# Three more groups of the modulation products on TensorE, in a two-block kernel on one core

## The chip, the cores and the metric

The kernel runs on one core of a Trainium2 chip. The metric is the device time of one execution in microseconds; smaller is better. A core has five engines with an instruction queue each: TensorE (PE; its weight loads are shown as PEld), VectorE (DVE), ScalarE (ACT), GpSimd (POOL) and SyncE (SP), which here only issues the large loads. All run their own queue in order and wait for each other on semaphores.

## The reference

A token stream x (256 tokens, width 1024) goes through two layers of a first block and one layer of a second; a context stream of 256 tokens goes beside it. Each layer begins with modulation vectors that depend on a conditioning vector alone:

```python
mod = (jax.nn.silu(c) @ ada_w[i] + ada_b[i])[:, None, :]
sh1, sc1, g1, sh2, sc2, g2 = jnp.split(mod, N_MOD, axis=-1)
hx = modulate(rms_norm(x, norm_mix[i]), sh1, sc1)      # h * (1 + scale) + shift
...                                                    # the same with c_ctx for the context
m_lat, m_ctx = hybrid_mixer(hx, hc, ...)               # layer 0: attention heads beside a state-space scan
x = x + g1 * m_lat
x = x + g2 * swiglu(modulate(rms_norm(x, norm_ffn[i]), sh2, sc2), ...)
```

Layer 1 has a short convolution in place of the hybrid mixer. The second block does the same with its own weights (w_mod_2), a mixer of two linear recurrences and a mixture of experts. Each modulation product is a vector of 1024 against a matrix of 1024 × 6144 in fp32, 24 MB; there are three matrices. Only the shift and scale ahead of the first mixer of each block are wanted for c and for c_ctx; all others for c alone.

## The kernel before

**The modulation products.** A matrix is taken in three groups of 2048 columns, so there are nine groups (m, s): m is the matrix (0 and 1 for the two layers of the first block, 2 for the second block) and s the third of its columns. A group is eight tiles of 128 rows by 2048 columns, 1 MB each, one for each eighth (kt) of the contraction. `gemv(m, s)` loads a tile into the buffer `raw` and multiplies it in one of two ways. With `both` true, TensorE multiplies it by `csil`, 128 × 32 with silu(c) and silu(c_ctx) in its first two columns, and adds up over the eight tiles in a bank `gv`; the four slices of 512 columns go to four groups of 32 output partitions (four matmuls in the program, eight records in the trace). With `both` false, VectorE multiplies the tile by a column of `csil` and adds it to an accumulator `gva` of 128 × 2048, in two halves (L331 for the first tile, L333 for the others), and four matmuls against ones at the end of the group sum over the partitions, into the same kind of bank. In both cases L341 adds the bias on VectorE and gives `gvr`. `gv_cols` transposes `gvr` to columns, `gv_row` writes a gate to memory, from where `bc_row` reads it back.

**Who asks for them.** `gemv` is a generator: it yields after each tile. The first group (0,0) runs at the start. The others come in the order (0,1), (0,2), (2,0), (1,0), (1,1), (1,2), (2,1), (2,2), a tile at a time, where `pump` is called: some calls between the input projections of the first mixer (`hybrid`), three for each of its sixteen attention heads until the scan `ssd` is done, and after that together with the context side of the second block, beside the output projection, the first feed-forward part and so on. A scheduler then puts the instructions of each engine in an order of its own; loads on SP stay in the order in which the program asks for them.

**The buffers.** `raw` has three buffers, shared by the tiles of the modulation products and all slices of weights of the first block and the context side. A slice of weights is split into two halves of higher and lower bits (`split_to`: L243 on ScalarE and VectorE, into `whl`, three buffers), and three products (`mm3`) take the place of one. A load waits until the buffer's last reader is done.

**The mixer around it.** The slices of hy_w_in come in the order of the convolution part (bands of `xbc`), k and v, q, and z. For each head TensorE makes the scores `sc`, VectorE the maximum `nb`, ScalarE the exponential `e` with its sum `l`, VectorE the scaling (L714), TensorE four transposes of `e` (L731); four heads share a product `pv`. Beside them the scan has products `st`, `rb` and `yo`, and elementwise work on `g`, `mf`, `mb`, `xw` on VectorE. After the heads the norm of the context stream (`dg`, `hf`), its first projections (`c_hi`, `c_lo`) and the output projection (`mt_hi`, `mt_lo`) follow on TensorE.

Of the kernel before, what the change touches and what calls it, by code (L numbers as in the profile page):

```python
# [141 lines left out]
def tile_model(ctx: ExitStack, tc: tile.TileContext, aps: dict, out: bass.AP, dbg=None):  # L142
# [46 lines left out]
    def bank(name="b", tag=None):  # L189
        t = tag or tagsel[0]  # L190
        return psum["pool"].tile([P, 512], F32, tag=t, name=name, bufs=psum["tags"][t])
# [30 lines left out]
    def mm(o, l, r, start=True, stop=True):  # L222
        return nc.tensor.matmul(o, l, r, start=start, stop=stop)  # L223
# [86 lines left out]
    def gemv(m, s):  # L310

        w, cn = MATS[m]
        both = s == 0 and m != 1
        for i in range(1 + both):
            nc.gpsimd.dma_start(gvb[i:i + 97:32, :], aps["bias"][m, s])
        o = bank("gv", "G") if both else None
        acc = None if both else gvp.tile([P, 2048], F32, tag="gva", name="gva", bufs=1)
        for kt in range(KT):  # L320
            raw = ring.tile([P, 2048], F32, tag="raw", name="raw", bufs=NRAW)
            dmas.append(nc.sync.dma_start(raw, w[kt * P:(kt + 1) * P, s * 2048:(s + 1) * 2048]))
            if both:
                for g in range(4):
                    mm(o[32 * g:32 * g + 32, :], csil[cn][:, kt, :], raw[:, g * 512:(g + 1) * 512], kt == 0,
                       kt == KT - 1)
            else:
                for h in range(2):
                    c = slice(h * 1024, (h + 1) * 1024)
                    if kt == 0:  # L330
                        nc.vector.tensor_scalar(acc[:, c], raw[:, c], csil[cn][:, kt, 0:1], None, op0=ALU.mult)  # L331
                    else:
                        nc.vector.scalar_tensor_tensor(acc[:, c], raw[:, c], csil[cn][:, kt, 0:1], acc[:, c],  # L333
                                                       op0=ALU.mult, op1=ALU.add)
            yield
        if not both:
            o = bank("gv", "G")
            for g in range(4):
                mm(o[32 * g:32 * g + 32, :], ones[:, :32], acc[:, g * 512:(g + 1) * 512])
        r = gvp.tile([P, 512], F32, tag="gvr", name="gvr", bufs=1)  # L340
        nc.vector.tensor_add(r, o, gvb)  # L341
        return r
# [30 lines left out]
    def mods(m, parts):  # L373

        for i in parts:
            r = yield from gemv(m, i)
            if i == 0:
                MOD[f"c1_{m}"] = gv_cols(r, 1 if m == 1 else 2, f"ma{m}")
            elif i == 1:
                MOD[f"g1_{m}"] = gv_row(r, 0, f"g1_{m}")  # L380
                MOD[f"sh2_{m}"] = gv_cols(r, 1, f"mb{m}")[0][:, 8:16]
            else:
                MOD[f"sc2_{m}"] = gv_cols(r, 1, f"mc{m}")[0][:, 0:8]
                MOD[f"g2_{m}"] = gv_row(r, 1, f"g2_{m}")
# [1719 lines left out]
```

## Time and profile before

| | |
|---|---|
| time, median of 3 runs | 1550.29 us (1550.26 to 1551.28) |
| the profiled execution | 1556.02 us, of it the span from first to last instruction 1554.2 |
| TensorE busy | 1407.8 us (91%), 8039 matmul records |
| VectorE busy | 955.1 us (61%) |
| ScalarE busy | 634.8 us (41%) |
| GpSimd busy | 157.3 us (10%) |
| granted TensorE clock, mean | 0.943 of full speed |
| read from HBM | 317.37 MB |

The profile comes from one execution; its engines' busy times say nothing yet of who waits for whom. The granted clock has two levels, 1.00 (2.4 GHz) and 0.50 (1.2 GHz); a value between them is a mean over a stretch. A busy time at the lower level holds half the work. Times in the rows below are microseconds from the start of the span, unless marked ns.

### The profile page before, as it was taken

How to read it: one execution, taken by the hardware profiler on the slowest of the kernel's cores; microseconds unless marked ns; L12 is line 12 of the kernel's file. 1: busy time of each engine (PE TensorE's matmuls, PEld its weight loads, DVE VectorE, ACT ScalarE, POOL GpSimd, SP SyncE). 2: the span in 40 equal slices, each digit the busy share in tenths (PEclk: the TensorE clock that was granted, in tenths of full speed). 3: DMA queues.
4: the chain of work that ended last, by engine and by line, in shares of the span. 5: the costliest groups of instructions: out<-in, count | busy, mean ns of one | idle time of the engine just before them, and what ended most of it. 6: DMA issues, size and time to landing. Idle time of an engine off the chain costs nothing. (4 is left out here: it accounts for less than half of the span.)

```text
span 1554.2 us, 20809 instructions
## 1 busy us (share of the span) xinstructions
PE 1407.8 (91%) x8039; PEld 1061.2 (68%) x8039; DVE 955.1 (61%) x1526; ACT 634.8 (41%) x1020; POOL 157.3 (10%) x213
## 2 busy tenths in 40 slices
PE   4988698999999999999999997988899897989996
PEld 2666445677787798997788886888797753444442
DVE  1577869786888977755455566799944532223232
ACT  2643234554555435344444444864641411111211
POOL 2013220000001000001000000134402100000000
PEclk9997798999999999999999997999897978999998
DMA  9444558787789842443355552323210696999990
GB/s 353 161 152 139 200 209 307 245 293 260 268 279 328 299 154 96 136 136 130 128 189 189 180 182 94 128 83 108 82 55 1 229 340 227 362 358 388 393 355 29
DMA packets 133471, 320.35 MB, mean 206 GB/s; under 512 B 6632, under 2 KB 25064, under 8 KB 124112
## 3 DMA queue, kind: packets, MB, share of 16 engines
q1 hardware_dynamic: 130848, 311.31, 56.8%
q0 software_dynamic: 2480, 7.16, 1.3%
q8 instruction: 86, 1.41, 0.4%
q14 instruction: 57, 0.47, 0.1%
HBM read 317.37 MB, written 1.07 MB: 205 GB/s over the span
## 5 line engine op out<-in xcount | busy, mean ns | idle before, releaser
L243 DVE TENSOR_TENSOR whl<-raw,whl 128x1024 fp32r<-128x1024 f32 x252 | 311.1, 1242 | 179.2 <-ACT whl L243 178.7
L243 ACT CAST whl<-raw 128x1024 fp32r<-128x1024 f32 x252 | 261.8, 1047 | 320.2 <-PE b L223 115.3
L223 PE MATMUL gu<-whl,f_hi 128*128 128x512 f32 (+1 forms) x768 | 230.4, 383 | 1.8 <-DVE whl L243 1.8
L223 PEld LDWEIGHTS gu<-whl,f_hi 128*128 128x128 f32 x768 | 139.6, 189 | 34.7 <-DVE whl L243 3.4
L223 PE MATMUL gu<-whl,f_lo 128*128 128x512 f32 (+1 forms) x384 | 144.3, 377 | 0.0
L333 DVE SCALAR_TENSOR_TENSOR gva<-raw,csil,gva 128x1024 f32<-128x1024 f32 x98 | 123.4, 1291 | 16.9 <-DMA raw<-in_ada_w_dram 16.7
L223 PE MATMUL do<-whl,th 128*128 128x512 f32 x352 | 114.0, 400 | 0.3 <-DVE whl L243 0.2
L223 PE MATMUL gu<-mw,xg 128*64 128x512 f32 x384 | 91.7, 629 | 13.4 <-PEq L1964 11.2
L223 PEld LDWEIGHTS gu<-whl,f_lo 128*128 128x128 f32 x384 | 72.6, 189 | 14.2 <-issue 0.5
L223 PE MATMUL b<-l_hi,whl 128*128 128x256 f32 x384 | 75.4, 296 | 5.5 <-DVE whl L243 5.5
L223 PEld LDWEIGHTS gu<-mw,xg 128*64 128x64 f32 x384 | 32.7, 144 | 69.7 <-issue 65.7
L223 PEld LDWEIGHTS do<-whl,th 128*128 128x128 f32 x352 | 65.8, 188 | 17.0 <-DVE whl L243 1.8
L223 PE MATMUL b<-s_hi,whl 128*128 128x256 f32 x384 | 73.3, 287 | 0.0
L223 PE MATMUL do<-whl,tl 128*128 128x512 f32 x176 | 69.1, 396 | 0.0
L223 PEld LDWEIGHTS b<-l_hi,whl 128*128 128x128 f32 x384 | 61.9, 196 | 8.4 <-DVE whl L243 5.9
L223 PEld LDWEIGHTS b<-s_hi,whl 128*128 128x128 f32 x384 | 60.4, 189 | 0.7 <-issue 0.7
L223 PE MATMUL b<-whl,l_hi 128*128 128x512 f32 x160 | 52.8, 409 | 5.5 <-DVE whl L243 4.1
L1930 DVE SCALAR_TENSOR_TENSOR yf<-dn,gs,gbc 64x512 f32<-64x512 f32 (+1 forms) x36 | 25.9, 720 | 51.8 <-PEq L1964 47.7
L1282 DVE SCALAR_TENSOR_TENSOR qkv<-raw,cols_sb,qkv 128x189 f32<-128x189 f32 (+3 forms) x112 | 56.6, 551 | 0.0
L1891 DVE TENSOR_TENSOR sl<-sl,gu 128x256 f32<-128x256 f32 (+1 forms) x17 | 7.0, 413 | 79.4 <-ACT sl L1890 79.4
L223 PE MATMUL b<-l_lo,whl 128*128 128x256 f32 x192 | 55.6, 290 | 0.0
L223 PE MATMUL b<-s_lo,whl 128*128 128x256 f32 x192 | 54.9, 286 | 0.0
(549 smaller groups left out, 2723.6 us busy)
## 6 DMA issues: line engine op xcount, KB each, us to landing
raw<-in_ada_w_dram SPq DMA_DIRECT2D x48, 1024.0 KB, 5.1
raw<-in_w_in_dram SPq DMA_DIRECT2D x28, 1024.0 KB, 4.9
raw<-in_w_mod_dram SPq DMA_DIRECT2D x24, 1024.0 KB, 5.0
mw<-in_w_gate_dram SPq DMA_DIRECT2D x48, 512.0 KB, 12.2
mw<-in_w_up_dram SPq DMA_DIRECT2D x48, 512.0 KB, 11.5
raw<-in_ffn_w_gate_dram SPq DMA_DIRECT2D x22, 1024.0 KB, 5.1
raw<-in_ffn_w_up_dram SPq DMA_DIRECT2D x22, 1024.0 KB, 5.0
mw<-in_w_down_dram SPq DMA_DIRECT2D x22, 1024.0 KB, 11.9
```

The lines of the kernel that those rows point to most:

```text
L223: return nc.tensor.matmul(o, l, r, start=start, stop=stop)
L243: return nc.scalar.copy(hi, src), nc.vector.tensor_sub(lo, src, f32(hi))
L333: nc.vector.scalar_tensor_tensor(acc[:, c], raw[:, c], csil[cn][:, kt, 0:1], acc[:, c], op0=ALU.mult, op1=ALU.add)
L1282: nc.vector.scalar_tensor_tensor(yy, ov[:, r0 + dr:r1 + dr, c0 + dc:c1 + dc], c[:, 3 * a + b:3 * a + b + 1], yy, op0=ALU.mult, op1=ALU.add)
L1891: s2 = nc.vector.tensor_mul(sl[:, :c], sl[:, :c], o[:, c:2 * c])
L1930: nc.vector.scalar_tensor_tensor(yv, o[v, :c], gs[v, :], g2[v, n * c:(n + 1) * c], op0=ALU.mult, op1=ALU.mult)
```

## The change

Whether a group goes to TensorE is decided by the flag `both`. It was true for (0,0) and (2,0), the two groups that are wanted for both vectors. It is now true for (0,1), (0,2) and (1,0) too. The number of bias loads, which hung on `both`, now has the old condition written out, so it stays as it was.

```diff
         w, cn = MATS[m]
-        both = s == 0 and m != 1
-        for i in range(1 + both):
+        both = (m, s) in ((0, 0), (0, 1), (0, 2), (2, 0), (1, 0))
+        for i in range(2 if s == 0 and m != 1 else 1):
             nc.gpsimd.dma_start(gvb[i:i + 97:32, :], aps["bias"][m, s])
         o = bank("gv", "G") if both else None
         acc = None if both else gvp.tile([P, 2048], F32, tag="gva", name="gva", bufs=1)
```

The program's lists of instructions have 48 elementwise instructions fewer on VectorE; on TensorE 96 matmuls against `csil` more and 12 against ones fewer. The two lists of SP have the same loads in the same order. In the changed kernel lines from 314 on are numbered one higher.

On TensorE, between the k and v projection of the first mixer and its q projection, stood before the state products `st`, the transposes of k (L633) and the scan's `rb`:

```order
L223 MATMUL st<-xw,bt 64x256 x12
L633 MATMUL b<-cst,k_767 128x128 x2
L223 MATMUL rb<-cst_72,da 128x128 x4
L633 MATMUL b<-cst,k_800 128x128 x2
L223 MATMUL rb<-cst_72,da 128x128 x2
```

The same place now has the second to the fifth tile of group (0,1) in it:

```order
L223 MATMUL gv<-raw,csil_86 32x512 x8
L223 MATMUL st<-xw,bt 64x256 x8
L223 MATMUL gv<-raw,csil_86 32x512 x4
L223 MATMUL st<-xw,bt 64x256 x4
L634 MATMUL b<-cst,k_769 128x128 x2
L223 MATMUL rb<-cst_72,da 128x128 x4
L634 MATMUL b<-cst,k_802 128x128 x2
L223 MATMUL rb<-cst_72,da 128x128 x4
L223 MATMUL gv<-raw,csil_86 32x512 x4
```

Four matmuls (x4) are one tile; the tiles two and three stand ahead of the state products, the fourth between them, the fifth behind the second `rb`.

On SP's queue the loads of the last slices of hy_w_in and of the fourth to sixth tile of (0,1) alternate; in brackets stands whose work frees the buffer (the second name; the first is the queue of the buffer's earlier load). Before:

```order
L248 DMA raw<-in_hy_w_in_dram 128x4x512 [waits DMAHW2_49,DVE_49]
L322 DMA raw<-in_ada_w_dram 128x2048 [waits DMAHW7_49,DVE_49]
L248 DMA raw<-in_hy_w_in_dram 128x4x512 [waits DMAHW4_49,DVE_49]
L322 DMA raw<-in_ada_w_dram 128x2048 [waits DMAHW1_49,DVE_49]
L248 DMA raw<-in_hy_w_in_dram 128x4x512 [waits DMAHW6_49,DVE_49]
L322 DMA raw<-in_ada_w_dram 128x2048 [waits DMAHW3_49,DVE_49]
```

And now:

```order
L248 DMA raw<-in_hy_w_in_dram 128x4x512 [waits DMAHW1_49,DVE_49]
L323 DMA raw<-in_ada_w_dram 128x2048 [waits DMAHW0_49,PE_49]
L248 DMA raw<-in_hy_w_in_dram 128x4x512 [waits DMAHW2_49,PE_49]
L323 DMA raw<-in_ada_w_dram 128x2048 [waits DMAHW4_49,PE_49]
L248 DMA raw<-in_hy_w_in_dram 128x4x512 [waits DMAHW6_49,PE_49]
L323 DMA raw<-in_ada_w_dram 128x2048 [waits DMAHW3_49,DVE_49]
```

Four of the six loads that waited for VectorE now wait for TensorE.

On VectorE, in the first heads of the attention, the accumulation of group (0,2) stood between the softmax (`nb`, `e`, `l`) and the scan (`g`, `mb`):

```order
L333 SCALAR_TENSOR_TENSOR gva<-raw,csil_86,gva 128x1024 x2
L240 COPY pt<-b 128x4x128
L714 TENSOR_SCALAR e<-e,l 128x512
L898 SCALAR_TENSOR_TENSOR mf<-g,dt,cst_72 128x128 x2
L333 SCALAR_TENSOR_TENSOR gva<-raw,csil_86,gva 128x1024
L708 TENSOR_REDUCE nb<-sc 128x1
L879 TENSOR_SCALAR g<-rb,cum 128x128 x2
L333 SCALAR_TENSOR_TENSOR gva<-raw,csil_86,gva 128x1024
```

On TensorE the same heads now hold the tiles of (0,2), the first three of them (eleven matmuls and, further down, the twelfth) behind the first two heads' scores:

```order
L223 MATMUL gv<-raw,csil_86 32x512 x11
L223 MATMUL rb<-cst_72,da 128x128
L223 MATMUL yo<-mf,xt 64x128
L223 MATMUL yo<-e,s_0_814 64x128
L223 MATMUL yo<-e,s_1_781 64x128
L223 MATMUL rb<-cst_72,da 128x128
L223 MATMUL yo<-mf,xt 64x128
L223 MATMUL gv<-raw,csil_86 32x512
L732 MATMUL b<-cst,e 128x128 x4
L223 MATMUL sc<-kd_591,qT 128x512
```

From here to the end of the group (1,0) a tile or two stand between the heads, and after the heads between the products of the context's norm and projection.

## Rows read from the trace of the kernel before

**Rows 1.** Windows: stretch, then PE, PEld, DVE, ACT, POOL busy, as headed.

```profile
core 0: us, PE busy (x) PEld busy (x) DVE busy (x) ACT busy (x) POOL busy (x), PEclk, DMA share, GB/s
38.00:100.00 62.00, 57.47 (x305) 45.87 (x306) 38.99 (x58) 36.90 (x54) 3.14 (x11) 0.94 0.51 178
...
160.00:182.00 22.00, 14.82 (x67) 8.17 (x65) 18.35 (x37) 7.41 (x16) 4.08 (x7) 0.78 0.50 167
182.00:200.00 18.00, 13.10 (x37) 6.00 (x38) 16.31 (x30) 3.12 (x7) 6.78 (x8) 0.51 0.78 254
200.00:234.00 34.00, 33.91 (x175) 13.74 (x174) 20.85 (x58) 11.48 (x26) 6.70 (x13) 1.00 0.55 207
234.00:252.00 18.00, 12.98 (x54) 6.70 (x52) 15.42 (x32) 7.74 (x17) 1.45 (x3) 0.97 0.88 337
252.00:260.00 8.00, 6.58 (x20) 4.24 (x20) 8.00 (x15) 4.07 (x6) 0.00 (x0) 0.50 0.87 297
...
260.00:292.00 32.00, 31.83 (x141) 22.17 (x139) 21.21 (x29) 13.78 (x19) 2.33 (x3) 0.98 0.82 266
```

**Rows 2.** Waits of TensorE in 160 to 205: total, times, longest.

```profile
PE yo L223 <- DVE l L713: 6.5, 1, 6.5
PE b L731 <- DVE e L714: 4.5, 2, 2.3
```

**Rows 3.** Windows of the instructions on gva alone (PE, PEld, DVE busy).

```profile
160.00:205.00 45.00, 2.99 (x12) 0.35 (x12) 19.37 (x16) 0.70 0.59 199
...
234.00:260.00 26.00, 0.00 (x0) 0.00 (x0) 12.43 (x11) 0.82 0.88 325
```

**Rows 4.** The tile gva: ns min/median/max, first and last start.

```profile
L333 DVE SCALAR_TENSOR_TENSOR gva<-raw,csil,gva x98: 1259/1277/1975, 61.4 to 540.1; 128x1024 f32<-128x1024 f32 x98
...
L331 DVE TENSOR_SCALAR gva<-raw,csil x14: 742/745/761, 49.1 to 490.7; 128x1024 f32<-128x1024 f32 x14
```

**Rows 5.** TensorE in order of time: start, length, what, count, idle before.

```profile
10.47 1.93 PE L223 MATMUL gv<-raw,csil 128*32 128x512 f32 x8 [10.47 <-DMA raw<-in_ada_w_dram]
...
163.70 1.07 PE L223 MATMUL gv<-gva,cst 128*32 128x512 f32 x8
...
209.30 2.78 PE L223 MATMUL gv<-raw,csil 128*32 128x512 f32 x24
...
216.14 1.06 PE L223 MATMUL gv<-raw,csil 128*32 128x512 f32 x8
217.13 0.66 PE L347 MATMUL b<-cst,gvr 128*128 128x128 f32 x4
...
231.75 1.92 PE L223 MATMUL gv<-raw,csil 128*32 128x512 f32 x16
```

**Rows 6.** VectorE in order of time, three pairs on gva.

```profile
103.23 2.47 DVE L333 SCALAR_TENSOR_TENSOR gva<-raw,csil,gva 128x1024 f32<-128x1024 f32 x2
...
133.08 2.88 DVE L333 SCALAR_TENSOR_TENSOR gva<-raw,csil,gva 128x1024 f32<-128x1024 f32 x2
...
141.39 2.46 DVE L333 SCALAR_TENSOR_TENSOR gva<-raw,csil,gva 128x1024 f32<-128x1024 f32 x2
```

**Rows 7.** TensorE in order of time, two of its waits.

```profile
106.45 0.65 PE L223 MATMUL st<-xw,bt 128*64 128x256 f32 x4 [3.49 <-DVE xw L844]
...
144.51 1.11 PE L663 MATMUL b<-cst,qr 128*128 128x128 f32 x4 [3.31 <-DVE qr L599]
```

**Rows 8.** SP's queue in order of time (merged rows: start, from first to last).

```profile
1.64 23.38 SPq L322 DMA_DIRECT2D raw<-in_ada_w_dram  x8
...
127.23 59.10 SPq L322 DMA_DIRECT2D raw<-in_ada_w_dram  x11
...
267.66 0.33 SPq L322 DMA_DIRECT2D raw<-in_ada_w_dram  x1
```

**Rows 9.** The tile raw, last line of the view.

```profile
DMA to landing us min/median/max: 3.7/5.1/15.1
```

## The prediction

> **What bounds the kernel now.** I read the busy time of the engines by stretch first, then who waits for whom, then the rows of TensorE and VectorE in order of time. The granted clock stands beside the busy time, and that matters here: a matmul at the lower of the two levels takes twice as long and looks just as busy. So I count TensorE's work as busy time times granted clock. In the heads of the first mixer the stretches 160–182 and 182–200 hold 14.82 × 0.78 + 13.10 × 0.51 = 18.2 us of work in 40 us: 21.8 us are lost to idling and to the low clock [rows 1]. VectorE is busy 18.35 of 22 and 16.31 of 18 there. In 200–234 the same heads go on with TensorE busy 33.91 of 34 at clock 1.00 and VectorE at 20.85 of 34: nothing is lost. What differs is the accumulation into gva, 19.37 us of VectorE in 160–205, and what TensorE waits for there is VectorE: 6.5 us on the softmax sum l, 4.5 us on the scaled scores e [rows 2, 3]. 234–260 is of the same kind: 12.98 × 0.97 + 6.58 × 0.50 = 15.9 us of work in 26, 10.1 lost, with 12.43 us of gva on VectorE [rows 1, 3]. In 38–100 (57.47 of 62) and 260–292 (31.83 of 32) TensorE is the bound. So the first mixer is bound by VectorE in two pieces and by TensorE around them.
>
> **The change, part by part.** I call the tiles of group (0,1) a1 to a8, of (0,2) b1 to b8, of (2,0) c1 to c8, of (1,0) d1 to d8. The a, b and d tiles change engine; c was on TensorE already, and (1,1), (1,2), (2,1), (2,2) stay.
>
> Removed from VectorE: 48 instructions, 42 of 1.28 us and 6 of 0.75 us, some 58 us [rows 4]; two consecutive ones advance by about 2.4. Removed from TensorE: three closing sums over partitions, 1.07 us each at the full clock [rows 5]; I take 1.0 for the start-to-start step.
>
> Added on TensorE: 24 tiles of eight records. Their price is in the trace, since (0,0) and (2,0) do the same: three tiles in a run 2.78 us, one by itself from 216.14 to the next start at 217.13, so 0.99; at the low clock 1.93 [rows 5]. I take 1.0 for each, as they mostly stand alone. The Trainium skill, TensorEngine Tiling (Array Packing), Key Properties, says that a change of tiling mode drains TensorE, which speaks against scattering 24 such tiles among full-width products; here the whole difference between alone and in a run is 0.99 against 0.93, so the drain is at most 0.06 us a tile, 1.5 us in all, and the 1.0 already holds it.
>
> *Term 1, the rotary stretch, +3.3.* At 144.51 TensorE had waited 3.31 us for qr of VectorE [rows 7]. Ahead of qr on VectorE stand a6 and a7, 2.88 and 2.46 us [rows 6]: 5.3 less. On TensorE a6 and a7 now stand ahead of it: 2.0 more. Bounds 0 and +5.3.
>
> *Term 2, up to the q projection, −1.0.* a1 falls where TensorE is full: −1.0. a2 to a5 (4.0 us) go in around the state products, where TensorE waited 3.49 us for xw [rows 7], and VectorE loses the pair at 103.23, 2.47 us, just ahead of xw [rows 6]. These I take as even. But the order on SP's queue shows a new wait: the loads of a4, h6, a5 and h7 (h for the slices of hy_w_in) are now released by TensorE, because a tile's buffer comes free when its product has run, and a2's product runs only behind the kv projection. a4 can be issued then, and lands 5.1 us later (median) [rows 9]; its product stands between eight and four of the state products, which wait behind it, and behind them the transposes of k and all of the q projection. The eight state products and the wait for xw cover about 3 us of it. Lower bound −6.1 (one landing in full), upper +2.
>
> *Term 3, the heads, +12.8.* 21.8 us are lost in 160–200. VectorE keeps the softmax, as in 200–234, where nothing is lost; I leave 3 us for the first head's chain (max, exponential, sum, scaling), which has only part of the b tiles to hide it. TensorE gets b1 to b8, 8.0, and loses two closing sums, 2.0. So 21.8 − 3 − 6.0 = 12.8. Bounds: 9 left over gives +6.8, nothing left over +15.8.
>
> *Term 4, from the last heads to the output projection, +0.1.* 10.1 lost in 234–260, again 3 left over; d1 to d8 cost 8.0 and one closing sum goes, 7.0 in all, three of the tiles falling into the full stretch 260–292. 10.1 − 3 − 7.0 = +0.1. Bounds: −7 if none of the loss comes back, +3.1.
>
> Bias: its additions and DMAs are the same in number; nothing. GpSimd's queue, which loads the bias and writes the gate rows to memory, moves with gvr, and its first reader, the output projection, comes over 100 us behind (0,1). Loads: the same in number and in the same order on SP. Eight in a row took 23.38 us, 2.9 each [rows 8]; the 27 from a6 to d8 need 79 us and have some 125 (before, from 127.23 to 267.66 [rows 8], less what is gained), so their rate is no bound. The bank for gv is now held over a whole group, but nobody else uses its tag.
>
> Behind the output projection the order of all engines is the old one but for a few neighbours that swap, and each piece starts when its predecessor lets it, so what is gained there is kept to the end.
>
> Sum: 3.3 − 1.0 + 12.8 + 0.1 = 15.2 us. Against the profiled execution, 1556.0 us (span 1554.2 and 1.8 around it), that is 1540.8; the median of the runs shown is 5.7 us under that execution, so 1550.3 − 15.2 = **1535.1 us**.
>
> **Rivals.** *More comes back (0.17):* nothing is left over in terms 3 and 4 (+6.0), and term 1 gets its 5.3 (+2.0): 1527.1. For it speaks the full row at 200–234, which has products of this kind in it; the new ones also fill gaps that let the clock fall. The Trainium skill, TensorE: Matmul & The Clock Gate, What's actually happening, says the clock is reduced by default and activity releases it; the trace agrees, with 0.51 in the idle heads and 1.00 in the filled ones.
>
> *Less comes back (0.14):* the softmax chain, not VectorE's load, holds the heads, and 9 us stay lost: 1541.1. Against it: VectorE's rows in 182–200 are back to back.
>
> *No change (0.08):* the 16 tiles b and d run at the low clock, 1.93 for 1.0, +14.9: 1550.0. It needs the heads to stay as broken up as now.
>
> *Slower (0.11):* TensorE takes its matmuls in order, so a gate tile that has not landed stops all behind it; its buffer is freed by TensorE's own earlier gate product, and the loop closes. A full landing costs 5.1 us [rows 9]. It decides from three full landings on (15.3 us against 15.2). The places are a4, a5, a8, b4 and d6, each waiting for a buffer that a product frees; all five in full: +25.5, 1560.6. Against it: counting the products between the freeing one and the waiting one, b4 to c8 have about 5 us or more between them.
>
> **How the numbers follow.** The forecast itself has 0.50, its own range 1529 to 1541. Changes within 0.2% (3.1 us) are about what a measurement of this kernel cannot tell from none. Faster: 0.50 + 0.17 + 0.14 = 0.81; same 0.08; slower 0.11. All upper bounds together give 5.3 + 2 + 15.8 + 3.1 = 26.2, so 1524.1, and I go 2 us lower because busy times clock is only a measure of work; upwards the range takes in no change: 1522 to 1550.
>
> **What would show it.** After: no gva on VectorE before some 265 us; TensorE's clock near 1.00 through all heads, and busy with hardly a gap; the last c tile's product some 14 us earlier (before, the second half of the sixteen records at 231.75 [rows 5]); the output projection some 15 us earlier, and the same distance from there on. Wrong: TensorE idle ahead of gv records with a DMA as releaser (the slower rival); heads that still wait for l and e with VectorE idle (less comes back); gv records of 1.9 us for eight in the heads (no change).

## The result and the profile after

| | before | changed |
|---|---|---|
| median of the runs | 1550.78 us (1550.26 to 1551.42, 4 runs) | 1529.23 us (1523.67 to 1532.29, 4 runs) |
| ratio, 95% interval | | 0.9854 (0.9829 to 0.9879) |
| a second time, beside new runs of before | 1552.7 us (1547.27 to 1565.9, 17 runs) | 1528.49 us (1522.4 to 1534.56, 6 runs), 0.9846 (0.9805 to 0.9887) |
| span of the profiled execution | 1554.2 us | 1528.8 us, the second time 1522.2 us |
| TensorE busy, mean clock | 1407.8 us, 0.943 | 1405.3 us, 0.964 |
| VectorE busy | 955.1 us | 903.6 us |

The changed kernel is faster by 21.5 us where 15.2 were forecast (1535.1); 1529.2 lies inside the range of 1522 to 1550. The interval of the ratio lies clear of 1 both times.

The windows of the changed kernel, in the stretches of [rows 1]:

```profile
core 0: us, PE busy (x) PEld busy (x) DVE busy (x) ACT busy (x) POOL busy (x), PEclk, DMA share, GB/s
38.00:100.00 62.00, 58.44 (x300) 45.22 (x301) 31.04 (x47) 37.05 (x53) 0.00 (x0) 0.94 0.35 115
160.00:182.00 22.00, 22.00 (x116) 9.06 (x114) 14.08 (x43) 9.57 (x21) 2.60 (x6) 1.00 0.77 284
182.00:200.00 18.00, 18.00 (x112) 7.95 (x110) 13.23 (x38) 6.59 (x16) 5.58 (x11) 1.00 0.67 255
200.00:234.00 34.00, 33.02 (x176) 14.19 (x173) 20.07 (x58) 14.22 (x29) 4.44 (x9) 1.00 0.77 281
234.00:252.00 18.00, 18.00 (x93) 10.52 (x93) 11.05 (x21) 8.33 (x11) 1.35 (x2) 1.00 0.62 221
252.00:260.00 8.00, 7.25 (x40) 4.07 (x38) 2.53 (x3) 3.17 (x4) 0.00 (x0) 1.00 1.03 374
```

From 160 to 200 TensorE is busy 40.00 of 40 us at clock 1.00, where 21.8 us were lost [rows 1]. The waits of TensorE from the rotary stretch to the end of the heads, in the changed kernel (total, times, longest):

```profile
PE gv L223 <- DMA raw<-in_ada_w_dram: 1.2, 2, 0.8
PE b L223 <- DVE dg L434: 1.0, 1, 1.0
PE b L664 <- DVE qr L600: 0.9, 1, 0.9
```

The waits for l and e of [rows 2] are gone, and that for qr has fallen from 3.31 us [rows 7] to 0.9. The tile gva in the changed kernel (ns min/median/max, first and last start): nothing of it stands ahead of 264.1 us.

```profile
L334 DVE SCALAR_TENSOR_TENSOR gva<-raw,csil,gva x56: 1270/1276/1965, 276.8 to 521.3; 128x1024 f32<-128x1024 f32 x56
...
L332 DVE TENSOR_SCALAR gva<-raw,csil x8: 743/746/753, 264.1 to 472.0; 128x1024 f32<-128x1024 f32 x8
```

**Where the time came from.** Six points of the program are the same work in every kernel: the first `cb` product of the scan, the first transposes of qr, the first product on mt_hi (output projection), the first and the last transposes tt of the feed-forward, the first product of the experts (gu from mw). I call the stretches between them A (up to the rotary transposes), B (heads, context, up to the output projection), C (output projection, start of the feed-forward), D (feed-forward), E (recurrences and routing), F (experts). The windows of before cut at these points, in the order A to F:

```profile
86.70:144.50 57.80, 42.98 (x245) 32.59 (x244) 43.87 (x88) 21.89 (x44) 14.38 (x20) 0.86 0.37 130
144.50:291.90 147.40, 128.62 (x600) 76.15 (x601) 110.44 (x221) 54.39 (x102) 24.05 (x38) 0.86 0.69 240
291.90:366.20 74.30, 69.87 (x322) 53.77 (x320) 65.28 (x87) 45.97 (x63) 3.25 (x6) 1.00 0.77 263
366.20:931.30 565.10, 554.04 (x3206) 476.62 (x3206) 383.99 (x495) 254.95 (x345) 24.46 (x34) 0.99 0.58 195
931.30:1255.30 324.00, 287.09 (x1901) 256.42 (x1899) 232.53 (x404) 161.81 (x287) 76.93 (x75) 0.90 0.31 110
1255.30:1554.20 298.90, 261.67 (x1477) 124.41 (x1477) 83.15 (x181) 57.60 (x120) 1.63 (x5) 0.95 0.81 303
```

The same of the changed kernel:

```profile
88.20:142.30 54.10, 47.29 (x298) 32.83 (x297) 34.80 (x81) 22.60 (x46) 12.26 (x20) 0.94 0.47 158
142.30:272.30 130.00, 126.75 (x709) 69.53 (x709) 74.30 (x190) 52.00 (x97) 19.15 (x39) 1.00 0.75 267
272.30:348.90 76.60, 69.98 (x319) 53.69 (x319) 64.45 (x83) 47.22 (x66) 3.26 (x6) 1.00 0.78 265
348.90:912.50 563.60, 553.08 (x3205) 475.42 (x3206) 384.47 (x495) 255.32 (x346) 23.60 (x34) 0.99 0.58 196
912.50:1237.20 324.70, 287.89 (x1901) 257.05 (x1900) 232.57 (x404) 161.93 (x288) 76.96 (x75) 0.90 0.31 110
1237.20:1528.80 291.60, 255.83 (x1477) 122.15 (x1477) 83.17 (x181) 57.60 (x120) 1.61 (x4) 0.97 0.83 310
```

B is 17.4 us shorter and A 3.7, C is 2.3 longer; D and E are within 1.5 us of before. F is 7.3 shorter, though the change touches nothing there: the same 1477 records took TensorE 5.8 us less, at clock 0.97 after 0.95. With lost time counted as in the prediction (length less busy times clock), B had 147.4 − 128.62 × 0.86 = 36.8 us lost and now has 130.0 − 126.75 × 1.00 = 3.2, for 16.2 us more work on TensorE.

### The profile page after: what moved, and what is told of

It reads as the page before. It is cut to its first block, busy times and chain, and to the rows that moved or that the text cites. A ratio compares the mean times of both kernels' runs of the same rounds, so it can differ in the third digit from the quotient of the medians.

```text
span 1528.8 us, 21093 instructions
## 1 busy us (share of the span) xinstructions
PE 1405.3 (92%) x8207; PEld 1051.9 (69%) x8207; DVE 903.6 (59%) x1478; ACT 635.0 (42%) x1020; POOL 149.0 (10%) x213
## 3 DMA queue, kind: packets, MB, share of 16 engines
q1 hardware_dynamic: 130848, 311.31, 57.4%
HBM read 317.37 MB, written 1.07 MB: 208 GB/s over the span
## 5 line engine op out<-in xcount | busy, mean ns | idle before, releaser
L223 PE MATMUL gu<-mw,xg 128*64 128x512 f32 x384 | 88.5, 610 | 9.7 <-PEq L1965 7.5
L334 DVE SCALAR_TENSOR_TENSOR gva<-raw,csil,gva 128x1024 f32<-128x1024 f32 x56 | 70.6, 1293 | 9.0 <-DMA raw<-in_ada_w_dram 9.0
L223 PE MATMUL gv<-raw,csil 128*32 128x512 f32 x320 | 46.9, 651 | 17.9 <-DMA raw<-in_ada_w_dram 17.9
```

## The experiments

Every kernel is the changed one with the edit shown. The table gives the lengths of A, B and C in the profiled execution, their sum, the sum against before (279.5), and the ratio of the runs to those of before with its interval.

| kernel | A | B | C | sum | against before | ratio |
|---|---|---|---|---|---|---|
| before | 57.8 | 147.4 | 74.3 | 279.5 | | |
| changed | 54.1 | 130.0 | 76.6 | 260.7 | −18.8 | 0.9854 (0.9829 to 0.9879) |
| changed, again | 53.9 | 128.8 | 78.9 | 261.6 | −17.9 | 0.9846 (0.9805 to 0.9887) |
| (0,1) alone | 50.9 | 143.7 | 74.0 | 268.6 | −10.9 | 0.992 (0.9891 to 0.9948) |
| (0,2) alone | 58.8 | 139.0 | 80.7 | 278.5 | −1.0 | 0.9998 (0.9973 to 1.0023) |
| (1,0) alone | 58.8 | 145.0 | 77.9 | 281.7 | +2.2 | 0.9966 (0.9941 to 0.9991) |
| (0,2), (1,0) | 57.4 | 136.8 | 77.9 | 272.1 | −7.4 | 0.9919 (0.9891 to 0.9947) |
| (0,1), (0,2) | 53.9 | 132.7 | 76.5 | 263.1 | −16.4 | 0.9834 (0.9806 to 0.9861) |
| both engines | 60.0 | 140.7 | 80.8 | 281.5 | +2.0 | 1.0005 (0.9978 to 1.0031) |
| a quarter | 50.2 | 127.6 | 78.3 | 256.1 | −23.4 | 0.9828 (0.9779 to 0.9877) |
| next to nothing | 52.0 | 129.0 | 75.8 | 256.8 | −22.7 | 0.9862 (0.9819 to 0.9904) |
| twice | 51.8 | 150.2 | 76.7 | 278.7 | −0.8 | 0.9977 (0.9959 to 0.9995) |
| with (1,1) | 50.9 | 130.0 | 81.4 | 262.3 | −17.2 | 0.9839 (0.9804 to 0.9874) |
| all nine | 50.8 | 130.5 | 79.6 | 260.9 | −18.6 | 0.9958 (0.9938 to 0.9979) |

The table counts from the first `cb` product. Ahead of it the same 296 records of TensorE took until 86.7 us in before and with (0,2) alone, and until 89.3 with (1,0) alone, so small differences from the start of the span say little. From the start of the span, (0,1) alone is 7.5 us ahead of before at the feed-forward (358.7 against 366.2), where the table has 10.9. In "a quarter" and "next to nothing" part of the products is left out, so the routing behind D gets other values, and their ratios do not compare the same work.

My theory after the result: what TensorE lost in the heads was due to VectorE's load, each group gives back its own part, and its products cost TensorE about 1.0 us a tile. Rivals: the groups only work together; or the products themselves, put into TensorE's gaps, hold its clock up, whatever VectorE does.

### One group at a time, and pairs

```diff
-        both = (m, s) in ((0, 0), (0, 1), (0, 2), (2, 0), (1, 0))
+        both = (m, s) in ((0, 0), (2, 0), (0, 1))            # or (0, 2), or (1, 0), or (0, 2), (1, 0)
```

(0,1) alone: 

> Of the three groups only (0,1) goes to TensorE. Theory (the gain is the load taken off VectorE where TensorE waits for it, so each group brings its own term and the terms add up): the scores of the first head came 2.95 us earlier in the changed kernel, 2.8 lost by the q projection and 5.7 won in the rotary stretch; nothing else changes, so -3 us, 1545 to 1550. Rival (the three groups only work together, because the loads run through one ring of buffers): 0 to -1. Rival (the loads that now wait for TensorE cost more than the rotary stretch gives): slower by 1 to 3.

(0,2) alone: 

> Of the three groups only (0,2) goes to TensorE. Theory: 21.8 us were lost in 160 to 200 and the tiles cost TensorE 6 net, so -13 to -16 us, 1535 to 1538, with TensorE at the full clock through the heads that hold the tiles and the loss in 234 to 260 still there. Rival (only together): under half of it, -3 to -8. Rival (the gain in the heads is really the earlier start that (0,1) gives): -0 to -3.

(1,0) alone: 

> Of the three groups only (1,0) goes to TensorE. Theory: 10.1 us were lost in 234 to 260 and the tiles cost 7 net: -0 to -4 us, 1547 to 1551; the heads at 160 to 200 stay as broken up as before. Rival (only together): slower by 3 to 7, since the cost is paid and the loss stays.

(0,2) and (1,0): 

> (0,2) and (1,0) go to TensorE, (0,1) stays with VectorE. Theory: the changed kernel less the 3 us of (0,1), so 16 to 19 us faster than before, 1532 to 1535. Rival ((0,1) costs as much as it gives, since its loads wait for TensorE among the state products): as fast as the changed kernel or faster, 1526 to 1529.

All four sizes were missed: the medians are 1540.98, 1550.48, 1545.72 and 1539.49 us. (0,1) alone brings 10.9 us up to the feed-forward where I gave it 3 (6.9 of them in A, where the changed kernel got 3.7; the clock of A stands in the last section). (0,2) alone brings 7.4 us up to the output projection (A and B), about half of what I gave it, and then loses 6.4 in C. So its time is the one of its second rival, but not for that rival's reason, since B is 8.4 us shorter without an earlier start. Its windows B and C:

```profile
145.50:284.50 139.00, 125.39 (x646) 72.44 (x646) 94.80 (x208) 52.27 (x99) 22.38 (x38) 0.93 0.71 249
284.50:365.20 80.70, 74.83 (x328) 58.31 (x328) 64.64 (x83) 47.71 (x66) 5.90 (x6) 0.96 0.73 252
```

and TensorE's waits from the end of B on for halves of weights that ScalarE makes, with the row at which the longest ends:

```profile
PE b L223 <- ACT whl L243: 6.7, 2, 4.0
```

```profile
284.54 0.50 PE L223 MATMUL b<-whl,mt_hi 128*128 128x512 f32 x1 [4.04 <-ACT whl L243]
```

The 4.04 us lie ahead of the first product on mt_hi, so they are the end of B; in C one such wait of 2.7 us is left, where before had none. Of the 6.4 us, 1.4 are more idling and 5.0 more busy time (74.83 after 69.87, at clock 0.96 after 1.00). Up to the output projection the terms do add up: A and B together are 10.6, 7.4 and 1.4 us shorter for the three alone, 19.4 in sum, against 21.1 and 22.5 with all three; so "only together" falls there. In C it seems to hold: (0,2) alone gives nearly all of its gain back there, and with (1,0) beside it about half as much (3.6). So I tried the other pair:

```diff
-        both = (m, s) in ((0, 0), (0, 1), (0, 2), (2, 0), (1, 0))
+        both = (m, s) in ((0, 0), (2, 0), (0, 1), (0, 2))
```

> (0,1) and (0,2) go to TensorE, (1,0) stays with VectorE. (0,2) alone was 7.4 us ahead at the output projection and 1.0 at the feed-forward, (0,2) with (1,0) 11.0 and 7.4 (counted from the first cb product). Theory (with the heads shorter, the accumulation of (1,0) falls beside the context's and the output projection, where VectorE also splits weights that TensorE waits for, so (1,0) is worth more beside (0,2) than alone): 10 to 13 us ahead of before at the feed-forward, 6 to 9 behind the changed kernel, 1535 to 1541. Rival (the terms add up, (1,0) is worth nothing): within 2 us of the changed kernel, 1527 to 1531.

My theory fell: by the table this pair is 1.5 to 2.4 us behind the changed kernel at the feed-forward, and it is not behind it at the end (1525.09 us median, 1523.92 to 1528.67, 5 runs). With (0,1) and (0,2) on TensorE, (1,0) is worth nothing that these runs can measure. It is the best median of the study, but the intervals of the ratios overlap, so it is not shown to beat the changed kernel.

### VectorE's load or TensorE's filled gaps

Both engines multiply the three groups, and VectorE's sums are not read:

```diff
-        acc = None if both else gvp.tile([P, 2048], F32, tag="gva", name="gva", bufs=1)
+        new = (m, s) in ((0, 1), (0, 2), (1, 0))
+        acc = None if both and not new else gvp.tile([P, 2048], F32, tag="gva", name="gva", bufs=1)
...
-            else:
+            if acc is not None:
```

> TensorE's work as in the changed kernel, VectorE's as before: the tiles of (0,1), (0,2) and (1,0) are multiplied on both engines, and VectorE's sums are not read. Theory (what is lost in the heads is due to VectorE's load): the loss comes back, the stretch from the rotary transposes to the output projection takes 145 to 160 us against 130.0, and the time is 1550 to 1565. Rival (it is the matmuls put into TensorE's gaps that keep its clock up, whatever VectorE does): 130 to 136 us there, 1529 to 1536.

The time is that of before (1553.64 against 1552.7 us), but not stretch by stretch: against before A is 2.2 us longer, B 6.7 shorter and C 6.5 longer. A and B together take 200.7 us; before 205.2, changed 184.1. Window B of this kernel, and its longest waits of TensorE there:

```profile
150.10:290.80 140.70, 129.03 (x695) 69.79 (x695) 110.38 (x221) 52.02 (x98) 28.45 (x38) 0.95 0.72 247
```

```profile
PE b L733 <- DVE e L716: 6.0, 4, 2.8
PE gv L223 <- DMA raw<-in_ada_w_dram: 4.4, 3, 1.9
```

The wait for e is back with VectorE's 110.38 us, and B is 10.7 us longer than in the changed kernel. But it is 140.7, not the 145 or more that the theory wanted: with VectorE loaded as in before, the filled gaps are worth 6.7 us, at clock 0.95 against 0.86. That the whole time falls on that of before is C's 6.5 us, and chance. One reservation: a tile's buffer is now held until both engines are done, which may explain the 4.4 us for loads (1.2 in the changed kernel), so not all of the 10.7 need be VectorE's load.

The opposite, VectorE relieved and TensorE given less, took two tries. First, one of a tile's four matmuls instead of four, for all but the first tile of a group:

```diff
-                for g in range(4):
+                new = (m, s) in ((0, 1), (0, 2), (1, 0))
+                for g in range(1 if new and kt else 4):
...
```

> VectorE relieved as in the changed kernel, but TensorE does a quarter of the new work: in (0,1), (0,2) and (1,0) only the first tile has its four matmuls, the other seven tiles one of four, so 15.75 of 24 us of new products are left out and the gates are not the reference's; the loads stay. Stages are compared up to the output projection and the feed-forward, since the routing behind depends on the values. Theory (VectorE's relief is the gain, the products only cost): the stretch from the rotary transposes to the output projection takes 118 to 122 us against 130.0, with the clock at 0.95 or more, and the feed-forward starts 12 to 15 us earlier than in the changed kernel. Rival (the products keep the clock up): the clock falls to 0.7 to 0.9 in that stretch and it stays at 127 to 135 us.

It tells nothing on the question, since it takes next to no time off TensorE (125.23 us busy in B after 126.75). A tile by itself in the quarter kernel, then one in the changed kernel:

```profile
136.36 1.04 PE L223 MATMUL gv<-raw,csil 128*32 128x512 f32 x2
```

```profile
137.31 1.07 PE L223 MATMUL gv<-raw,csil 128*32 128x512 f32 x8
```

One matmul takes as long as four: they go to four groups of output partitions and run side by side. The second try leaves one matmul of 32 columns:

```diff
+                if (m, s) in ((0, 1), (0, 2), (1, 0)) and kt:
+                    mm(o[:32, :32], csil[cn][:, kt, :], raw[:, :32], False, kt == KT - 1)
+                    yield
+                    continue
...
```

> The earlier cut to a quarter saved TensorE nothing, since a tile's four matmuls ran side by side (a single one 1.04 to 1.05 us, all four 1.06). Here seven of the eight tiles of (0,1), (0,2) and (1,0) get one matmul with 32 columns in place of four with 512; the rest of their product is left out, so the gates are not the reference's, and some 19 us of new work are taken off TensorE while loads and buffers stay as they are. Compared by stage up to the feed-forward. Theory (VectorE's relief is the gain, the products only cost): the stretch from the rotary transposes to the output projection takes 114 to 120 us against 130.0 and 128.8, clock 0.95 or more. Rival (the products put into the gaps keep the clock up): clock 0.7 to 0.9 there, 126 to 136 us.

Window B of this kernel, then 160 to 182 of it:

```profile
140.40:269.40 129.00, 120.51 (x622) 73.36 (x622) 74.22 (x191) 52.34 (x99) 20.58 (x39) 0.94 0.73 263
...
160.00:182.00 22.00, 19.41 (x92) 10.64 (x90) 14.94 (x45) 9.51 (x21) 4.34 (x10) 0.79 0.73 262
```

TensorE's work in B falls from 126.8 to 120.51 × 0.94 = 113.3 us, 13.5 less, and B stays at 129.0. The length is the rival's, the clock of 0.94 lies between the two. What the products no longer take is lost: 129.0 − 120.51 = 8.5 us idle (3.2 in the changed kernel) and 120.51 − 113.3 = 7.2 us to the low clock (none). So relief of VectorE alone brings the whole gain of B, and the products that replace its sums cost nothing there: without them 12.5 of the 13.5 us go to the low clock (7.2) and to idling (5.3 more). The idling is spread over waits of at most 1.2 us each. What would bound B below 129 is open; the loads are a candidate that no run here tests (the mean busy share of the DMA engines in B is 0.73).

B in the four cases, side by side: 147.4 us with VectorE loaded and without the new products (before), 140.7 loaded and with them, 129.0 relieved and with next to none, 130.0 and 128.8 relieved and with all. So VectorE's load is worth 18.4 us without the products and 10.7 beside them; the products are worth 6.7 us where VectorE is loaded, and nothing where it is relieved.

The clock is released by activity, says the Trainium skill, TensorE: Matmul & The Clock Gate, What's actually happening; the rows agree, 0.79 with the gaps in 160 to 182 and 1.00 with the products in them.

Every new product made twice:

```diff
-                for g in range(4):
+                new = (m, s) in ((0, 1), (0, 2), (1, 0))
+                for i in range(1 + new):
+                    for g in range(4):
...
-        nc.vector.tensor_add(r, o, gvb)
+        nc.vector.scalar_tensor_tensor(r, o, 0.5 if (m, s) in ((0, 1), (0, 2), (1, 0)) else 1.0, gvb,
+                                       op0=ALU.mult, op1=ALU.add)
```

> The changed kernel with every new product made twice (and the sum halved where the bias is added), so 24 us more of matmuls on TensorE, 16 of them in the heads and behind, and VectorE as in the changed kernel. Theory (the heads are now bound by TensorE, a tile costs its 1.0 us): the stretch from the rotary transposes to the output projection takes 143 to 147 us against 130.0 and 128.8, the end comes 16 to 24 us later, 1545 to 1553. Rival (there is still room for such products in TensorE's gaps): under 136 us there, under 1538.

The records on gv in window B of the changed kernel, and of this one:

```profile
142.30:272.30 130.00, 27.89 (x200) 4.60 (x200) 2.75 (x4) 1.00 0.75 267
```

```profile
145.30:295.50 150.20, 49.95 (x336) 9.71 (x336) 2.76 (x4) 1.00 0.67 233
```

22.06 us more of records make B 20.2 us longer than in the changed kernel: once TensorE is full, a product costs its whole time. The end comes 18.5 us later than in the changed kernel (median 1546.97), within what I expected; B does not, since 17 tiles fall into it and each second pass took 1.3 us, not 1.0. Part of that is the order, which splits tiles: four records by themselves take 1.05 us (at 177.09) where eight take 1.06. In A the six doubled tiles cost about 1 us: 51.8 us, where a single pass took 50.9 and 50.8 at the same clock of 1.00 (with (1,1), and all nine). The rival of free room falls in B.

### More groups

```diff
-        both = (m, s) in ((0, 0), (0, 1), (0, 2), (2, 0), (1, 0))
+        both = (m, s) in ((0, 0), (0, 1), (0, 2), (2, 0), (1, 0), (1, 1))    # or all nine
```

> The changed kernel with a sixth group, (1,1), on TensorE; its tiles lie beside the output projection and the first part of the feed-forward, where TensorE lost only 6.6 of 76.6 us. Theory (a group pays only where TensorE waits for VectorE): the eight tiles cost 8.0 and one closing sum goes, so 3 to 7 us slower than the changed kernel, 1533 to 1537. Rival (VectorE's load also holds the weights' splitting there, which TensorE waits for now): as fast or up to 4 us faster.

> All nine groups on TensorE. The sixth cost nothing that could be measured at the end (1528.9 against 1528.5) and 3 to 5 us in its stretch; the other three lie beside the feed-forward, 350 to 532, where TensorE lost 2 to 4 us of 183. Theory (a group costs TensorE 7 us where nothing is lost): 15 to 21 us slower than the changed kernel, 1543 to 1550, nearly all of it between 350 and 532. Rival (VectorE's splitting of weights holds TensorE there, and its relief pays as in the heads): within 5 us of the changed kernel.

(1,1) makes C 2.5 to 4.8 us longer than in the changed kernel, as the theory says, and D 1.9 to 3.7 (567.3). It has 3 us less in A, which is a matter of the clock (last section), and the time is the same (1528.91): the figure is the rival's, the stretches are the theory's. With all nine, D is the stretch that grows: 578.4 us against 563.6 and 565.4 in the changed kernel, 13 to 15 more, and the time is 1543.93 us, 15.4 above 1528.49. Windows C and D of it:

```profile
267.70:347.30 79.60, 79.60 (x398) 56.18 (x397) 45.81 (x66) 47.84 (x66) 2.84 (x6) 1.00 0.77 261
347.30:925.70 578.40, 570.61 (x3345) 476.98 (x3344) 335.11 (x449) 255.89 (x345) 22.43 (x34) 0.99 0.57 190
```

VectorE has 49.4 us less to do in D than in the changed kernel (335.11 against 384.47), and nothing is gained by it: TensorE was full (570.61 us busy of 578.40).

### The same kernel again

> The changed kernel once more, beside more runs of the kernel before, to see how far the same program varies and where. In the first two traces it was 19 us ahead at the first product of the output projection and 25 at the end. Theory (the change acts in the first mixer alone, the rest of the difference is variation of the last stage, routing and experts): again 17 to 21 us ahead at the output projection, another figure at the end, ratio 0.985 to 0.990. Rival (the change also speeds the last stage up): 24 to 26 us ahead at the end again.

```profile
88.70:142.60 53.90, 47.43 (x298) 32.96 (x297) 34.74 (x81) 22.64 (x46) 12.24 (x20) 0.94 0.47 158
142.60:271.40 128.80, 126.57 (x709) 69.69 (x710) 74.93 (x190) 52.71 (x97) 19.16 (x39) 1.00 0.75 268
271.40:350.30 78.90, 71.56 (x319) 54.80 (x317) 63.86 (x83) 46.37 (x66) 3.25 (x6) 0.98 0.76 260
350.30:915.70 565.40, 554.83 (x3205) 476.87 (x3206) 385.59 (x495) 255.46 (x346) 24.63 (x34) 0.99 0.58 195
915.70:1229.70 314.00, 275.07 (x1903) 247.91 (x1902) 232.61 (x404) 161.97 (x288) 77.89 (x75) 0.95 0.32 111
1229.70:1522.20 292.50, 256.39 (x1477) 122.39 (x1477) 83.01 (x180) 57.63 (x120) 1.61 (x4) 0.97 0.83 312
```

A and B repeat within 1.2 us. The output projection is 20.5 us ahead of before, the end of the feed-forward 15.6 (915.7 against 931.3). Then E takes 314.0 us at clock 0.95 where the same program took 324.7 at 0.90: 10.7 us that belong to no change, with 12.8 us less busy time of TensorE for the same work. The theory holds for the first mixer, and the end, 32.0 us ahead (1554.2 against 1522.2), is neither the rival's 24 to 26 nor the first execution's 25.4; the ratio came out a little below the 0.985 to 0.990 of the theory.

## Why the prediction was right, and where it was not

**Terms 1 and 2, +3.3 and −1.0: the sum was right, by luck.** The rotary transposes come 2.2 and 1.9 us earlier (144.5 against 142.3 and 142.6); +2.3 was forecast. The parts were off in opposite ways: the q projection starts at 122.41 after 119.59, so term 2 is −2.8, and term 1 about +5.0, near its bound. Term 1 counted VectorE's load alone. The windows from the q projection to the rotary transposes, of before and of the changed kernel, have the clock in it too:

```profile
119.60:144.50 24.90, 18.70 (x74) 13.46 (x72) 16.21 (x24) 5.72 (x8) 8.93 (x10) 0.77 0.36 127
```

```profile
122.40:142.30 19.90, 18.12 (x85) 12.33 (x84) 10.43 (x18) 6.40 (x10) 6.06 (x8) 0.91 0.47 161
```

The idle time falls from 6.2 to 1.8 us, the loss to the low clock from 4.3 to 1.6, and the work grows by 2.1; the 2.7 us of the clock are what the term left out. Of term 2's −2.8, 1.5 stand already at the first `cb` product (88.2 after 86.7), where the same program varies by more. The other 1.3 lie behind it, where the changed kernel took 34.2 us up to the q projection after 32.9. There the fourth tile of (0,1) and the state products behind it ran at the low clock in the changed kernel:

```profile
109.06 1.86 PE L223 MATMUL gv<-raw,csil 128*32 128x512 f32 x8
110.85 1.93 PE L223 MATMUL st<-xw,bt 128*64 128x256 f32 x8
```

and at the full one in the kernel with (1,1), whose list of TensorE is the same up to the context's projection, and which took 32.5 us:

```profile
108.83 1.07 PE L223 MATMUL gv<-raw,csil 128*32 128x512 f32 x8 [0.30 <-DMA raw<-in_ada_w_dram]
109.83 1.08 PE L223 MATMUL st<-xw,bt 128*64 128x256 f32 x8
```

At the full clock a2 to a5 thus come out as even (32.5 us after 32.9), but against a kernel that itself lost 1.9 us to the low clock there (24.28 us busy at 0.92).

**Terms 3 and 4, +12.9 together: too small; B gained 17.4 and 18.6.** Three sizes were off. The loss that could come back was 36.8 us in all of B; I had counted 31.9, from the two stretches where it was plain. I left 6 over; 3.2 and 2.2 stayed. The work added was 16.2, not 13.0: the tile a8, whose product stands at 143.36 behind the rotary transposes, is in no term (1.0), and the tiles in B took 1.12 us on the mean (27.89 for 25) where 1.0 was taken. 4.9 + 2.8 − 3.2 = 4.5, which is 17.4 − 12.9. What held the heads was VectorE's load, as forecast: relieving it alone takes B to 129.0, and giving it back beside the products takes B to 140.7. That the products are a cost to be set against the gain was a wrong picture in B, though the sum by busy times clock came out: taking them away gains nothing (129.0), only adding more costs (150.2). Split by group, (1,0) beside the other two is worth 2.7 to 3.9 us in B and nothing at the end; term 4 had +0.1.

**What is gained is kept to the end: wrong by 2.3 to 4.6 us.** C is 76.6 and 78.9 us after 74.3: the step that nothing is lost behind the heads failed. TensorE idles 6.6 us in C of the changed kernel after 4.4, and it now waits for halves of weights from ScalarE (the first of the three waits, 1.11 us, ends where C begins):

```profile
PE b L223 <- ACT whl L243: 3.8, 3, 1.6
```

ScalarE itself had waited for loads there: 3.11 us for hy_w_out up to its split at 282.64, and 6.54 for w_in up to that at 302.34; TensorE's waits of 1.56 and 1.13 us end 1.1 us behind the start of each. The likely reason is that the heads are shorter, and the loads for the projections behind them, in order on SP, come late instead. That was not tested, nor whether it is the buffers of raw or the transfer rate. In the second execution the low clock adds to it (71.56 us busy at 0.98, so 1.4).

Up to the feed-forward the changed kernel is thus 17.3 and 15.9 us ahead (366.2 against 348.9 and 350.3), and 15.2 were forecast: one term too small and one wrongly left out nearly cancel, which is luck again. The medians are 21.5 and 24.2 us apart, so some 4 and 8 us lie behind. There the profile of before, from an execution 5.2 us above its median, had both a long E (324.0; two others have 324.0 and 324.7, the rest 314.0 to 319.6) and the longest F of all profiles (298.9; the others 291.6 to 296.1). Most of the 7.3 us in F is busy time at a lower clock, as said above; TensorE's waits for its own sequencer, at the line of a branch, are 13.6 us in F of before and 11.4 in the changed kernel.

E varies by 10.7 us between two executions of one program, F by 0.9 there. By the profiles every kernel but the one with all nine groups is 3 to 16 us further ahead of before at the end than at the feed-forward, and there is one profile of before to hold them against; whether a few us of the change are earned there is open.

**The rivals.** "More comes back" (1527.1) described B rightly, with 2 to 3 us left over and clock 1.00, and lies nearest the median, nearer than the forecast. But at the feed-forward its 23.2 us are further off than the forecast's 15.2 (17.3 and 15.9 measured); it is E and F that bring the median to it. "Less comes back" and "no change" are out: no wait for l or e, gv records of 1.06 us in the heads. (The 1.93 us that "no change" takes for the low clock was read at 10.47, where the profile gives the clock as 1.00; the row at 109.06 above, 1.86 with the clock at 0.67 from 110 to 114, bears the size out.) "Slower" has its mechanism, at a small price: three waits for landings, 1.3 us in all, where three full ones (15.3) would have decided.

## What to carry to other kernels

Look for the stretch in which an engine loses time to another, count the loss over the whole stretch as length less busy times clock, and move work there only: the same move gained 18 us beside the heads, nothing beside the output projection, and with the feed-forward's groups moved too it lost 15, since TensorE was full there. Work put into gaps of TensorE can be free, as it was in the heads here: with 13.5 us of them left out, 12.5 went to the low clock and to idling. That ended when the gaps were full, and 22.06 us more of records cost 20.2. After a large gain in one stretch look at the next one: here the loads and weight splits that had time before were the new wait.

## What the runs showed of the hardware

Four matmuls with 32 stationary columns that go to four groups of output partitions took 1.06 to 1.07 us together and 1.04 to 1.05 for one. The Trainium skill, TensorEngine Tiling (Array Packing), Key Properties, says that tiles operate independently and can load and multiply in parallel; the rows agree.

The same list of TensorE's instructions in A met the low clock in three executions (A 53.9 to 54.1 us at 0.94: the changed kernel twice, and (0,1) with (0,2)), less of it in one (50.9 at 0.97: (0,1) alone) and none in two (50.9 and 50.8 at 1.00: with (1,1), and all nine). Between the changed kernel and the one with (1,1) the busy time in A is 47.29 and 44.31 us, the idle time 6.8 and 6.6. Between the two executions of the changed kernel the busy time in E is 287.89 and 275.07 us, the idle time 36.8 and 38.9. So three microseconds at one place and 10.7 at another go with the clock and with no change of the program, and a change of a few microseconds has to be read stretch by stretch.
